# A fused streaming-encoder block: seven products for 34 more weight units

## The chip, the cores and the metric

One core of one Trainium2 chip runs the whole kernel. The time is device microseconds from one launch, as the median of several runs. TensorE does the matrix products into PSUM, the accumulator memory, which this kernel uses as four tiles of 2 x 512 float32 columns for each partition. VectorE, ScalarE and GpSimd do elementwise work, and the queue of SyncE (SP) issues the loads and stores. Each engine works through its own instructions in a fixed order and waits on semaphores where it needs another engine's result.

## The reference

The reference is one encoder layer over 256 tokens of 2048 channels, all float32:

```python
x = x + 0.5 * swiglu(rms_norm(x, ffn1_norm), ffn1_w_gate, ffn1_w_up, ffn1_w_down)   # 2048 -> 5632 -> 2048
h = rms_norm(x, mix_norm); proj = h @ w_in                # pool group, and gated linear attention
x = x + concatenate([y_pool, y_gla]) @ w_out              # 2048 x 2048
x = x + mem_cross_attention(rms_norm(x, xattn_norm), rms_norm(mem, mem_norm), w_q, w_kv, w_o)
x = x + 0.5 * swiglu(rms_norm(x, ffn2_norm), ffn2_w_gate, ffn2_w_up, ffn2_w_down)
out = rms_norm(x, final_norm)

def swiglu(h, w_gate, w_up, w_down):
    return (silu(h @ w_gate) * (h @ w_up)) @ w_down
```

Some 417 MB are read from memory, nearly all of it weights, each once.

## The kernel before

Every weight matrix is cut into **units** of 1 MB (128 partitions x 2048 float32). A unit is loaded into a buffer `raw` (three of them); ScalarE rounds it to `wh` (line 228) and VectorE makes the remainder `wl = raw - wh` (line 229). Both are in the type fp32r, and there are three buffers of each. Activations are held as a high and a low part too: `xs` (the normed input) and `ys` (what goes into the next product). A float32 product is the sum of three: high x high, high x low, low x high (`products`, line 307).

The class `Stream` writes down the order of the work: units, and between them operations with a delay in units ("after 6 more units"). `emit` splits weights two units ahead of the products and issues the load three units ahead. A scheduler then fixes each engine's order of instructions; so it may place a matmul of a later unit before one of an earlier unit, or a cast ahead of an eviction.

A unit of a wide product (`wwide`) is two 128-row chunks of the weight by 1024 columns. With 256 tokens that is a 2 x 2 block product: 2 token halves, 2 chunks of the contraction, 2 column halves, three matmuls each, so 24 matmuls of 128x512. `block_t` does just that. It holds two PSUM tiles. `block_s` does some units of a block, the *pairs* 0, 2 and 4 of eight, by a scheme with **seven** instead of eight block products (Strassen-Winograd; `seven`, line 401): 21 matmuls. For these,

- `add_weights` (lines 363 to 367) makes four sums of the unit's quarters in `T`, and `split_seven` splits the 1536 columns of `raw` that are still needed (`xh`, `xl`) and the 2048 of `T`;
- `part_sums` (lines 346 to 356) makes four sums of the activation's quarters, split into `xe`;
- four PSUM tiles are held; two of them collect the four partial products P1, P5, P6, P7, which `combine` (lines 443 to 448) adds up in an SBUF tile `sg`, and the other two collect what belongs to the output directly; `join` (line 452) adds the two, from PSUM.

Before, `block_s` is used for the gate and up columns of both feed-forward networks except the first block and the odd last column (18 blocks, 54 units of seven products). The odd column's gate and up go together through `block_t` (`wtwo`). The down products, and the products with `w_out` and `w_o`, go through `into_x`: it fetches the residual `x` from memory (`fetch_x`), runs two blocks `block_t`, adds the product to `x` (line 608), stores it, and, where a norm follows, `fold` transposes `x` on TensorE (line 621) and writes the next `xs` (lines 210, 211). The feed-forward network runs in three parts of 4, 4 and 3 columns of 512; gated columns are transposed by `turn` (line 691) into `ys` and split (lines 234, 235). The very last down product has its own form, `down_end`, with line 1188.

Of the kernel before, what the change touches and what calls it, by code (L numbers as in the profile page):

```python
# [14 lines left out]
P = 128  # L15
# [77 lines left out]
def build(ctx, tc, I, out):  # L93
# [247 lines left out]
    def part_sums(act, ext, i, g):  # L341

        t = scope["pool"].tile([P, 4 * NB], F32, tag="T", name=uid("T"))
        a = t[:, :NB].rearrange("p (k s) -> p k s", k=2)
        e = t[:, NB : 2 * NB].rearrange("p (n s) -> p n s", n=4)
        nc.vector.tensor_tensor(
            out=a, in0=f32(act[:, 2 * g : 2 * g + 2, 0, :]), in1=f32(act[:, 2 * g : 2 * g + 2, 1, :]),
            op=ALU.add,
        )
        a11, a21, a12, a22 = (a[:, k, h * P : (h + 1) * P] for k in range(2) for h in range(2))  # L350
        nc.vector.tensor_tensor(out=e[:, 3], in0=a11, in1=a21, op=ALU.subtract)
        nc.vector.tensor_tensor(out=e[:, 1], in0=a22, in1=a21, op=ALU.subtract)
        nc.vector.scalar_tensor_tensor(
            out=e[:, 2], in0=e[:, 1], scalar=-1.0, in1=a11, op0=ALU.mult, op1=ALU.subtract
        )
        nc.vector.tensor_tensor(out=e[:, 0], in0=a12, in1=e[:, 2], op=ALU.add)
        split(ext[:, i, 0], ext[:, i, 1], e)
# [27 lines left out]
    def seven(banks, act, ext, i, g, first, later, weights):  # L385
# [3 lines left out]
        n4, n1, s2, s3 = ([ext[:, i, p, n] for p in range(2)] for n in range(4))  # L389
# [6 lines left out]
        order = ("P1", "P7", "P5", "P6", "P2", "P3", "P4") if first else (  # L396
            "P1", "P2", "P3", "P7", "P5", "P6", "P4")
        for n in order:
            (a, b), wh, wl = table[n]
            for j, (x, w) in enumerate(((a, wh), (a, wl), (b, wh))):  # L400
                nc.tensor.matmul(  # L401
                    banks[n], x, w, start=first and j == 0,
                    stop=not later and n in ("P1", "P5", "P6", "P7") and j == 2,
                )

    def block_s(srcs, act, ext, pairs, evict, delays=(0, 0)):

        held, n = {}, len(srcs)

        def open_banks():  # L410
            a, b, c, d = (ptile(uid("pt")) for _ in range(4))
            held["ps"] = (d, c)
            held["parts"] = (a, b)
            held["banks"] = {
                "P1": a[:, 0], "P6": a[:, 1], "P7": b[:, 0], "P5": b[:, 1],
                "P2": c[:, 0], "P4": c[:, 1], "P3": d[:, 0],
            }

        def unit_s(g):
            def fn(weights):  # L420
                if g == pairs[0]:
                    open_banks()
                seven(held["banks"], act, ext, pairs.index(g), g, g == pairs[0], g != pairs[-1],
                      weights)
            return fn

        def unit_p(g):
            def fn(wh, wl):
                wh, wl = (w.rearrange("p (k j n) -> p k j n", j=2, n=NB) for w in (wh, wl))
                for j in (1, 0):  # L430
                    for h in range(2):
                        for kk in range(2):

                            fresh = (j, h) == (0, 1) and g == min(set(range(n)) - set(pairs)) and kk == 0
                            products(held["ps"][j][:, h, :], act, 2 * g + kk, h, wh[:, kk, j],
                                     wl[:, kk, j], fresh, g == n - 1 and kk == 1)
            return fn

        def combine():
# [8 lines left out]
            nc.vector.tensor_tensor(out=e[:, 3], in0=b[:, 1], in1=e[:, 1], op=ALU.add)  # L448

        def join(j):  # L450
            e = held["e"][:, 0:2] if j else held["e"][:, 2:4]
            nc.vector.tensor_tensor(  # L452
                out=e, in0=held["ps"][j], in1=e, op=ALU.add if j else ALU.subtract
            )
            evict(j, e)

        for g, src in enumerate(srcs):
            if g in pairs:
                st.unit(src, unit_s(g), split_seven, add_weights)
                if g == pairs[-1]:  # L460
                    st.op(combine)
            else:
                st.unit(src, unit_p(g))
        for j in (1, 0):
            st.op(lambda j=j: join(j), delays[j])
# [138 lines left out]
    def residual(scale, b):  # L604

        def evict(j, ps):
# [4 lines left out]
            if j:  # L611
                store_x(b)
        return evict

# [15 lines left out]
    def into_x(w, act, scale, gain=None, k0=0, nk=KT, spread_too=True, src=None):  # L630

        for b in range(2):
            st.op(lambda b=b: fetch_x(b, src), 2)
            block_t(wwide(w, b * 2 * NB, k0, nk), act, residual(scale, b))
# [10 lines left out]
    PAIRS = (0, 2, 4)  # L645

    def pair_sums(g, delay):
        def f():
            if g == PAIRS[0]:
                rows["xe"] = scope["pool"].tile(  # L650
                    [P, len(PAIRS), 2, 4, P], F32R, tag="xe", name=uid("xe")
                )
            part_sums(xs, rows["xe"], PAIRS.index(g), g)
        st.op(f, delay)

    class Ext:


        def __getitem__(self, i):
            return rows["xe"][i]  # L660

    def ffn(wg, wu, wd, down):
        gate = {}

# [21 lines left out]
        def turn(g, k):  # L686
# [7 lines left out]
            split(ys[:, k : k + 4, 0, :], ys[:, k : k + 4, 1, :], v)  # L694

        for lo, n in FF_PARTS:
            for b in range(0, n - 1, 2):
                n0 = (lo + b) * NB
                if lo == b == 0:
                    block_t(wwide(wg, n0), xs, lambda j, ps: ev_gate(j, ps, 1))  # L700
                else:
                    block_s(wwide(wg, n0), xs, Ext(), PAIRS, lambda j, c: ev_gate(j, c, 0))
                block_s(wwide(wu, n0), xs, Ext(), PAIRS, ev_up)
                held = {}
                st.op(lambda held=held: held.update(gate))
                wait = PAIRS[-1] + 2 if b + 2 < n - 1 else 1
                for j in range(2):
                    st.op(lambda j=j, b=b, held=held: turn(held[j], 4 * (b + j)), wait)
            if n % 2:
                def both(j, ps):  # L710
                    if j:
                        ev_up(0, ps)
                    else:
                        ev_gate(0, ps, 1)
                block_t(wtwo(wg, wu, (lo + n - 1) * NB), xs, both)
                st.op(lambda n=n: turn(gate[0], 4 * (n - 1)), 1)
            down(wd, 4 * lo, 4 * n, lo + n == FF // NB)
# [10 lines left out]
    def down_first(wd, k0, nk, last):  # L728
        into_x(wd, ys, 0.5, G_MIX if last else None, k0, nk, src=None if k0 else I["x"][0])

    for g in PAIRS:
        pair_sums(g, 5)
    ffn(I["ffn1_w_gate"][0], I["ffn1_w_up"][0], I["ffn1_w_down"][0], down_first)
# [284 lines left out]
    st.op(open_scope("s_x"), 1)  # L1018


    xa = {}
# [33 lines left out]
    into_x(I["w_out"][0], ys, 1.0, G_X)  # L1055
# [80 lines left out]
    into_x(w_o, ys, 1.0, G_FFN2, spread_too=False)  # L1136
    st.op(close_scope, 1)
    st.op(open_scope("s_ffn2"), 1)
# [8 lines left out]
    def down_last(wd, k0, nk, last):  # L1147
        if last:
            down_end(wd, k0, nk)
        else:  # L1150
            into_x(wd, ys, 0.5, None, k0, nk)
# [86 lines left out]
    for n, g in enumerate(PAIRS):  # L1238
        pair_sums(g, 3 + n)
# [70 lines left out]
```

## Time and profile before

| | |
|---|---|
| median of 3 runs | 2134.21 us (2133.54 to 2135.17) |
| the profiled execution's own time | 2133.11 us |
| its span, first to last instruction | 2131.2 us |
| TensorE matmul busy | 2111.3 us (99%), 10032 instructions |
| weight load into TensorE (PEld) | 1768.5 us (83%) |
| VectorE busy | 1427.7 us (67%) |
| ScalarE busy | 1008.0 us (47%) |
| moved by DMA | 435.91 MB, mean 205 GB/s |

Rows of the timeline give the start, then the duration, then engine, line, operation and output<-inputs, with the idle time before it and what ended that in brackets. Rows of the groups give the count, then busy time and mean duration, then idle time before them. A matmul's duration in these rows is a modelled latency (0.39 us), while the distance from one matmul's start to the next is shorter; matmuls overlap. The same holds for VectorE: a row's duration is some 0.08 us longer than its distance to the next.

### The profile page before, as it was taken

Reading aid. Unit: us, or ns where it says so; the run is one execution under the profiler, and the core shown is the slowest. Engines: PE = TensorE matmul, PEld = TensorE weight load, DVE = VectorE, ACT = ScalarE, POOL = GpSimd, SP = SyncE. Lnnn points to the kernel's source line nnn. Section 1 sums busy time; section 2 is a strip of 40 time slices with the busy share of each in tenths; the row PEclk is TensorE's granted clock in tenths of the full one; section 3 lists DMA queues with packets and bytes.
Section 4 is the critical chain, followed back from the end, with each engine's and each line's share of the span. In section 5 each row is a group of like instructions: output and inputs, shape, how many; then the busy total and the mean of one; then the engine's idle time right before and its main releaser. Section 6 shows DMA issues by size and latency. Waiting matters only on the chain.

```text
span 2131.2 us, 24070 instructions
## 1 busy us (share of the span) xinstructions
PE 2111.3 (99%) x10032; PEld 1768.5 (83%) x10032; DVE 1427.7 (67%) x1189; ACT 1008.0 (47%) x890; POOL 14.2 (1%) x41
## 2 busy tenths in 40 slices
PE   9999999999999999999999999999999999999998
PEld 7878888888888888888888888888888888888886
DVE  8876588856864576565666454567874888658744
ACT  7554354534534545455445443445443455434433
POOL 0000000000000000000000000000000000000001
PEclk9999999999999999999999999999999999999999
DMA  7556665566656655557654555666576665766663
GB/s 277 197 189 234 224 221 195 186 233 226 227 178 234 221 162 180 167 185 278 222 190 161 167 169 171 195 207 207 175 247 217 214 209 175 249 212 223 221 217 119
DMA packets 143316, 435.91 MB, mean 205 GB/s; under 512 B 9828, under 2 KB 13000, under 8 KB 142824
## 3 DMA queue, kind: packets, MB, share of 16 engines
q1 hardware_dynamic: 143176, 434.38, 60.5%
q8 instruction: 78, 1.28, 0.2%
q14 instruction: 30, 0.25, 0.0%
q10 hardware_dynamic: 32, 0.01, 0.0%
HBM read 417.58 MB, written 16.78 MB: 204 GB/s over the span
## 4 chain that ended last, share of the span: by engine, by line
PE 98%; DVE 1%; issue 0%; ACT 0%; DMA 0%; SPq 0%; DVEq 0%; ACTq 0%
PE pt L307 58%; PE pa L292 15%; PE pt L401 12%; PE pb L307 6%; PE pe L307 3%; PE ph L691 1%; PE pl L1084 1%; PE pv L1119 1%; PE px L621 0%; DVE wl L229 0%; ACT wh L228 0%; DMA x<-in_x 0%; PE px L575 0%; PE po L954 0%; PE pa L832 0%
## 5 line engine op out<-in xcount | busy, mean ns | idle before, releaser
L229 DVE TENSOR_TENSOR wl<-raw,wh 128x2048 fp32r<-128x2048 f32 (+2 forms) x328 | 740.2, 2258 | 544.5 <-ACT wh L228 543.9
L228 ACT CAST wh<-raw 128x2048 fp32r<-128x2048 f32 (+2 forms) x328 | 618.5, 1886 | 721.7 <-PE pt L307 490.5
L307 PE MATMUL pt<-wh,xs 128*128 128x512 f32 x1952 | 618.6, 390 | 0.0
L307 PE MATMUL pt<-wh,ys 128*128 128x512 f32 x1728 | 534.7, 389 | 0.0
L307 PEld LDWEIGHTS pt<-wh,xs 128*128 128x128 f32 x1952 | 366.6, 188 | 75.7
L307 PE MATMUL pt<-wl,xs 128*128 128x512 f32 x976 | 380.8, 390 | 0.0
L307 PEld LDWEIGHTS pt<-wh,ys 128*128 128x128 f32 x1728 | 324.1, 188 | 67.0
L307 PE MATMUL pt<-wl,ys 128*128 128x512 f32 x864 | 336.3, 389 | 0.0
L292 PE MATMUL pa<-xs,wh 128*128 128x512 f32 x896 | 317.1, 398 | 2.1 <-DVE t L266 1.7
L292 PE MATMUL pa<-xs,wl 128*128 128x256 f32 x896 | 248.8, 281 | 0.0
L307 PEld LDWEIGHTS pt<-wl,xs 128*128 128x128 f32 x976 | 183.5, 188 | 37.9
L292 PEld LDWEIGHTS pa<-xs,wh 128*128 128x128 f32 x896 | 167.7, 188 | 41.2 <-issue 2.0
L307 PEld LDWEIGHTS pt<-wl,ys 128*128 128x128 f32 x864 | 162.2, 188 | 33.5
L292 PEld LDWEIGHTS pa<-xs,wl 128*128 128x128 f32 x896 | 169.2, 189 | 1.6 <-issue 0.2
L228 ACT CAST wh<-T 128x2048 fp32r<-128x2048 f32 x54 | 103.3, 1912 | 135.6 <-DVE T L367 93.3
L229 DVE TENSOR_TENSOR wl<-T,wh 128x2048 fp32r<-128x2048 f32 x54 | 123.6, 2288 | 65.3 <-ACT wh L228 65.3
L307 PE MATMUL pb<-wh,xs 128*128 128x512 f32 x384 | 121.7, 392 | 0.5 <-DVE ys L211 0.5
L401 PE MATMUL pt<-wh,xe 128*128 128x512 f32 x324 | 108.7, 389 | 0.0
L229 DVE TENSOR_TENSOR xl<-raw,xh 128x1536 fp32r<-128x1536 f32 x54 | 94.5, 1750 | 2.7 <-ACT xh L228 2.7
L228 ACT CAST xh<-raw 128x1536 fp32r<-128x1536 f32 x54 | 79.9, 1479 | 28.9 <-PE pt L401 28.8
L307 PEld LDWEIGHTS pb<-wh,xs 128*128 128x128 f32 x384 | 72.0, 188 | 15.6 <-DVE ys L211 0.7
L401 PE MATMUL pt<-xh,xs 128*128 128x512 f32 x216 | 78.6, 389 | 1.7 <-DVE sg L452 1.7
(203 smaller groups left out, 1666.3 us busy)
## 6 DMA issues: line engine op xcount, KB each, us to landing
raw<-in_ffn_w_down SPq DMA_DIRECT2D x88, 1024.0 KB, 5.5
raw<-in_ffn_w_up SPq DMA_DIRECT2D x80, 1024.0 KB, 5.0
raw<-in_ffn_w_gate SPq DMA_DIRECT2D x77, 1024.0 KB, 5.0
raw<-in_w_in SPq DMA_DIRECT2D x32, 1024.0 KB, 5.2
raw<-in_xattn_w_kv SPq DMA_DIRECT2D x32, 1024.0 KB, 5.2
raw<-in_w_out SPq DMA_DIRECT2D x16, 1024.0 KB, 6.2
raw<-in_xattn_w_q SPq DMA_DIRECT2D x16, 1024.0 KB, 5.2
raw<-in_xattn_w_o SPq DMA_DIRECT2D x16, 1024.0 KB, 5.6
```

The lines of the kernel that those rows point to most:

```text
L228: in_turn("scalar", lambda: nc.scalar.copy(hi, src))
L229: in_turn("vector", lambda: nc.vector.tensor_tensor(out=lo, in0=src, in1=f32(hi), op=ALU.subtract))
L292: nc.tensor.matmul(o, w, x, start=k == 0 and i == 0, stop=last and i == 1)
L307: nc.tensor.matmul(ps, a, w, start=first and i == 0, stop=last and i == 2)
L401: nc.tensor.matmul(banks[n], x, w, start=first and j == 0, stop=not later and n in ("P1", "P5", "P6", "P7") and j == 2,)
L691: nc.tensor.transpose(v[:, i, h * P : (h + 1) * P], g[:, h, i * P : (i + 1) * P], ident)
L1084: nc.tensor.matmul(ps[:, t, :M], ys[:, 4 * h + d, a, tok], xa["K"][:, d, b, :], start=i == 0, stop=i == 11,)
L1119: nc.tensor.matmul(ps[:, d, :S], xa["V"][:, m, a, col], xa["PT"][:, m, b, :], start=i == 0, stop=i == 5,)
```

## The change

`into_x` and the odd columns go through `block_s` too. In each of the 14 blocks of `into_x` two units have seven products (`Y_PAIRS`, pairs 0 and 2), in each of the two odd columns three: 14 x 2 + 2 x 3 = 34 units more, 88 in all. Which units come when is now given by a list: `ORDER` keeps the three at places 0, 2 and 4 of a block, `Y_ORDER` puts the two at 2 and 4, `Y_FIRST` (first block of `w_out` and `w_o`) at 4 and 6.

The sums of the activations become a class `Sums`. One of the four, S3, is written into `act` itself, over a quarter that the seven products do not read; the other three go to a tile of 3 planes instead of 4. For `ys` in the feed-forward networks, `turn` calls it with the transposed columns still in PSUM, which ScalarE copies; for `w_out` and `w_o` the sums are made from `ys`. In `into_x` the combined partial products are added to `x` by `early_parts`, two more operations of 128x1024, and `join` then adds the directly collected tiles as before. `w_out` and `w_o` have scopes of SBUF memory of their own, and the load and norm of `mem` comes after `w_out` instead of during it.

```diff
-    def part_sums(act, ext, i, g):
...
+    class Sums:
...
+        def make(self, g, src=None):
+            act, i = self.act, self.pairs.index(g)
+            if i == 0:
+                self.tile = scope["pool"].tile(
+                    [P, len(self.pairs), 2, 3, P], F32R, tag=self.name, name=uid(self.name)
+                )
+            a, e = jtile(), jtile().rearrange("p (n s) -> p n s", n=4)
+            k = slice(2 * g, 2 * g + 2)
+            if src is None:
+                nc.vector.tensor_tensor(
+                    out=a.rearrange("p (k s) -> p k s", k=2), in0=f32(act[:, k, 0, :]),
+                    in1=f32(act[:, k, 1, :]), op=ALU.add,
+                )
+            else:
+                nc.scalar.copy(a.rearrange("p (k s) -> p k s", k=2), src)
+            b = a.rearrange("p (n s) -> p n s", n=4)
+            nc.vector.tensor_tensor(
+                out=e[:, 0:2], in0=b[:, 0:4:3], in1=b[:, 1:2].to_broadcast([P, 2, P]), op=ALU.subtract
+            )
+            nc.vector.scalar_tensor_tensor(
+                out=e[:, 2], in0=e[:, 1], scalar=-1.0, in1=b[:, 0], op0=ALU.mult, op1=ALU.subtract
+            )
+            nc.vector.tensor_tensor(out=e[:, 3], in0=b[:, 2], in1=e[:, 2], op=ALU.add)
+            split(self.tile[:, i, 0], self.tile[:, i, 1], e[:, 1:4])
+            split(act[:, 2 * g, 0, P:], act[:, 2 * g, 1, P:], e[:, 0])
...
-    def block_s(srcs, act, ext, pairs, evict, delays=(0, 0)):
+    def block_s(srcs, act, sums, order, evict, merge=None):
...
+        def open_whole():
+            if "ps" not in held:
+                c = banks("P2", "P4")
+                held["ps"] = (banks("P3", "P0"), c)
+        def open_parts():
+            held["parts"] = (banks("P1", "P6"), banks("P7", "P5"))
...
+            if merge is not None:
+                merge(e[:, 2:4], e[:, 0:2])
         def join(j):
+            if merge is not None:
+                evict(j, held["ps"][j])
+                return
...
+    def early_parts(scale, b):
+        def merge(minus, plus):
+            for j, e, s in ((1, plus, scale), (0, minus, -scale)):
+                x = x_cols((2 * b + j) * NB, NB)
+                nc.vector.scalar_tensor_tensor(
+                    out=x, in0=e, scalar=s, in1=x, op0=ALU.mult, op1=ALU.add
+                )
+        return merge
...
-            block_t(wwide(w, b * 2 * NB, k0, nk), act, residual(scale, b))
+            block_s(wwide(w, b * 2 * NB, k0, nk), act, sums, orders[b], residual(scale, b, 0),
+                    early_parts(scale, b))
...
-    PAIRS = (0, 2, 4)
+    PAIRS, Y_PAIRS = (0, 1, 4), (0, 2)
+    ORDER = (0, 2, 1, 3, 4, 5, 6, 7)
+    Y_FIRST = (1, 3, 4, 5, 0, 6, 2, 7)
+    Y_ORDER = (1, 3, 0, 4, 2, 5, 6, 7)
+    CLEAR = 6
...
             split(ys[:, k : k + 4, 0, :], ys[:, k : k + 4, 1, :], v)
+            if not last:
+                for g in range(k // 2, k // 2 + 2):
+                    if g in Y_PAIRS:
+                        y_sums.make(g, v[:, 2 * g - k : 2 * g - k + 2])
...
-                block_t(wtwo(wg, wu, (lo + n - 1) * NB), xs, both)
+                block_s(wtwo(wu, wg, (lo + n - 1) * NB), xs, x_sums, ORDER, both)
...
+    def out_product(name, w, gain, spread_too):
+        sums = Sums("ye", ys, Y_PAIRS)
+        st.op(open_scope(name), 1)
+        for g in Y_PAIRS:
+            st.op(lambda g=g: sums.make(g), 1)
+        into_x(w, ys, 1.0, gain, spread_too=spread_too, sums=sums, orders=y_orders(KT, Y_FIRST))
+        st.op(close_scope, 1)
+    out_product("s_out", I["w_out"][0], G_X, True)
     st.op(open_scope("s_x"), 1)
...
     st.op(mem_norm, 6)
-    into_x(I["w_out"][0], ys, 1.0, G_X)
...
-    into_x(w_o, ys, 1.0, G_FFN2, spread_too=False)
     st.op(close_scope, 1)
+    out_product("s_o", w_o, G_FFN2, False)
```

147 lines of the change are left out of this document (70 added, 77 removed).

## The prediction

> **What bounds the kernel now.** I read the page's busy shares and the chain that ended last first.
>
> ```profile
> PE 2111.3 (99%) x10032; PEld 1768.5 (83%) x10032; DVE 1427.7 (67%) x1189; ACT 1008.0 (47%) x890; POOL 14.2 (1%) x41
> PE 98%; DVE 1%; issue 0%; ACT 0%; DMA 0%; SPq 0%; DVEq 0%; ACTq 0%
> ```
>
> TensorE is the bound: 98% of the chain. Its busy time alone would not prove that, as matmuls overlap, so the next view is its timeline in an up block.
>
> ```profile
> 312.56 0.39 PE L307 MATMUL pt<-wh,xs 128*128 128x512 f32 x1
> 312.79 0.39 PE L401 MATMUL pt<-xh,xs 128*128 128x512 f32 x1
> ...
> 317.32 0.39 PE L307 MATMUL pt<-wl,xs 128*128 128x512 f32 x1
> ```
>
> From 312.56 to 317.32 lie 21 starts (rows with x2 count twice): 4.76/21 = 0.2267 us for each matmul, in plain units and in seven-product units alike. Behind the start, what distances exceed that sums to under 9 us in the whole trace, the longest being 1.7 us idle. So each matmul removed is worth 0.2267 us where the operands keep coming. Whether they do is up to VectorE, which splits the weights. Its groups, then its timeline where it is tightest:
>
> ```profile
> L229 DVE TENSOR_TENSOR xl<-raw,xh 128x1536 fp32r<-128x1536 f32 x54 | 94.5, 1750 | 2.7 <-ACT xh L228 2.7
> L608 DVE SCALAR_TENSOR_TENSOR x<-pt,x 128x1024 f32<-128x1024 f32 x28 | 34.0, 1218 | 0.6
> ```
> ```profile
> 402.53 0.68 DVE L366 TENSOR_TENSOR T<-T,raw 128x512 f32<-128x512 f32 x1
> 403.25 0.69 DVE L367 TENSOR_TENSOR T<-T,raw 128x512 f32<-128x512 f32 x1
> 405.99 2.29 DVE L229 TENSOR_TENSOR wl<-T,wh 128x2048 fp32r<-128x2048 f32 x1 [2.05 <-ACT wh L228]
> 408.20 2.28 DVE L229 TENSOR_TENSOR wl<-raw,wh 128x2048 fp32r<-128x2048 f32 x1
> 410.40 1.22 DVE L363 TENSOR_TENSOR T<-raw 128x1024 f32<-128x1024 f32 x1
> 411.54 1.75 DVE L229 TENSOR_TENSOR xl<-raw,xh 128x1536 fp32r<-128x1536 f32 x1
> 413.21 0.68 DVE L366 TENSOR_TENSOR T<-T,raw 128x512 f32<-128x512 f32 x1
> 416.67 2.29 DVE L229 TENSOR_TENSOR wl<-T,wh 128x2048 fp32r<-128x2048 f32 x1 [2.05 <-ACT wh L228]
> ```
> ```profile
> 420.91 0.39 PE L401 MATMUL pt<-wl,xe 128*128 128x512 f32 x1
> ```
>
> From start to start an operation costs VectorE 2.20 us (2048 columns), 1.67 (1536), 1.13 (1024), 0.60 (512), some 0.4 (256) and 0.2 (128). In each seven-product unit it also idles up to 2.05 us while ScalarE casts `T`. The split that ends at 418.96 is first used at 420.91: a **lead** of 1.95 us, the smallest of its kind. In the down blocks the lead is 6.67 us.
>
> The last place is the end of the first network, where the product's last column must pass into the next `xs`:
>
> ```profile
> PE pt L401 <- DVE sg L452: 1.7, 1, 1.7
> ```
> ```profile
> 723.01 2.51 DVE L608 SCALAR_TENSOR_TENSOR x<-pt,x 128x1024 f32<-128x1024 f32 x2
> ```
> ```profile
> 729.74 1.91 PE L621 MATMUL px<-ident,x 128*128 128x128 f32 x16
> 731.40 0.48 PE L292 MATMUL pa<-xs,wh 128*128 128x512 f32 x1
> ```
>
> `x` was ready 4 us before the transposes asked for it. The first line is the only wait of TensorE for a PSUM tile in the 18 blocks with seven products.
>
> **The change, part by part.** *Removed:* 34 x 3 = 102 matmuls (the instruction order has 9978 before and 9876 after): 102 x 0.2267 = **-23.1 us**, all on the path.
>
> *VectorE's new work in a down block of 8 units:* for each of two units 1.13 + 0.60 + 0.60 + 1.67 = 4.0 us; `combine` 0.60 + 1.13 + 0.60 = 2.3; merge 2 x 1.13 = 2.3. With 8 splits (17.6) and two evictions (2.3) that is 32.5 us, and 36.6 with two waits of 2.05, against TensorE's 6 x 24 + 2 x 21 = 186 matmuls, 42.2 us. It fits, so it costs 0; without that cover it would be the 12.6 us new in each block. The same holds for `w_out` and `w_o` with their folds (8 x 0.4 = 3.2 more). ScalarE gets 34 x 1.4 + 16 x 0.5 + the sums, some 70 us on 1008: hidden, at 51%.
>
> *Sums of `ys`, 14 of them:* about 0.4 + 0.2 + 0.2 + 0.45 + 0.2 = 1.5 us of VectorE each, two to a part; in four places (parts one and two of both networks) they stand in front of the tight up block. In the new order they stand just where VectorE idled 2.05 us for the cast; two waits take the 3.0 us. Ends: 0, and 3.0 each = 12.0 with the idle time filled by nothing. I take 0, by the nearest row (the 2.05 us). Behind them in VectorE's queue are the splits of the next units, for which TensorE waits.
>
> *The odd columns:* 8 splits 17.6, three seven-product units 12.0, `combine` 2.3, join and gating of the block before 5.0: 36.9, and 43.0 with three waits, against 183 matmuls and 16 transposes, 43.1 us. Break-even: 0.
>
> *Down of 6 units in the first network's third part,* two blocks: 32.7 and 30.0 us of VectorE by the same prices with turns, sums and fold, plus two waits each: 36.8 and 34.1 against TensorE's 32.2 and 33.0. Overrun 5.7, against a lead of up to 6.7 at the start. The second block's splits stand behind eight operations of the fold, and following them in the new order the last plain unit's split comes 1.8 us late. I take **+1.8**; ends 0 and 5.7.
>
> *The boundary to `w_in`.* In the new order the twelve matmuls each of the last two seven-product units on P1, P5, P6, P7 stand behind nearly all of the last unit, because the folds hold the two PSUM tiles. So `combine` starts at the product's end E. Behind it, in VectorE's order: 0.60, 1.13, a split 2.20 (for which its cast ends at E + 1.9), 0.60, merge 1.13, split 2.20, 1.13, evictions 1.13 + 1.13: `x` is ready at E + 11.5. TensorE's two next units take 2 x 5.64, so the 16 transposes (1.66 from start to start) end at E + 13.2. ScalarE then has three squares (0.61 each), a cast (1.9), another square, and only then the scaled cast of `xs` (0.45): from E + 11.5 to 16.4. VectorE has one more split (2.20) in between, behind that cast, and reaches its part of `xs` at E + 18.1. TensorE's whole rest is queued behind that unit's first matmul. Before, it would start at E + 12.9: **+5.2**. Ends: 0 (if the scheduler's order proves earlier at `combine`) and 10.4 (if the other two norm boundaries did half as much each; there three plain units follow the last seven-product unit, and `x` is ready by E + 2.3, so I take 0).
>
> *Restart of TensorE after that wait.* The trace has two rows: after 1.70 us idle the next matmuls are 0.31 and 0.24 us apart; after the 4.13 us at the start they are 0.58, 0.42, 0.43, 0.43 and 0.41 apart, 1.1 us over five normal ones. The wait here, 5 us, is nearer the second: **+1.1**; ends 0 and 1.1. The granted clock reads 1.00 in both. [...]
>
> *PSUM.* All 16 new blocks hold four tiles, where `block_t` held two. One opening in 18 waited 1.7 us: 16/18 x 1.7 = **+1.5**; ends 0 and 16 x 1.7 = 27.2.
>
> *Moves at nothing.* The residual is needed from the merge on, not from the block's end; its load (5.6 us to landing) has three units, 16 us, ahead of it, and the weight load behind it in SP's queue waits for a later split anyway. The number of transfers is the same. Without cover: 5.6 each. The load and norm of `mem` fall among `w_q` units, where VectorE has one 2.2 us split per 5.64 us. The sums of `xs` in the first block move from its start to its end, where the lead is over 4 us; writing S3 must wait for the plain products, long done. Each at 0, with 1 us either way for the first block.
>
> *Sum:* -23.1 + 1.8 + 5.2 + 1.1 + 1.5 = -13.5, against the profiled execution's 2133.1 (2.0 beside its span): 2119.6. It lies 1.1 under the median of the runs shown, so **2120.7 us**.
>
> [...]
>
> **The rivals.** *All hidden* (2111.1): no term but the removal. For it, leads over 4 us nearly everywhere; against it, the order at the `w_in` boundary. 0.13. *VectorE's waits add up* (2125 to 2137, middle 2130): in the four tight up blocks new sums do not fall into idle time, 1.05 to 4.1 us each on top of the forecast. For it, a lead of only 1.95 there; against it, the order. 0.14. *PSUM openings, the slower one* (2146.4): every new block's opening waits like the one at 1.7 us: 2120.7 - 1.5 + 27.2. For it, four tiles of four are held and the transposes need two; against it, seventeen blocks in which nothing waits, and the new order, which puts products later rather than letting them wait. It decides from 12 of 16. 0.08. *No removal* is excluded by the count of instructions.
>
> **How the numbers follow.** The forecast's own case, 0.60, runs from 2115 to 2126. Within 0.2% (4.3 us, about what a measurement can tell from no change) is 2129.9 to 2138.5. Faster: 0.60 + 0.13 + the lower half of 0.14 + half of the 0.04 that no case holds = 0.82. Same: the upper half of 0.14, and 0.01 = 0.08. Slower: 0.08 + 0.02 = 0.10. The range 2111.5 to 2133 leaves out half of the case *all hidden* (0.06) below, and 0.08 + 0.02 and a third of 0.14 above.
>
> **What would show it.** Right: 102 matmuls fewer at the same 0.2267 us; an idle time of some 5 us of TensorE before the first `pa` matmul behind the transposes of `w_in`'s start, released by VectorE's `xs` of line 211; VectorE near 80%. Wrong: `pt` matmuls waiting for `wl` or for `x`/`sg` evictions at many block starts; or no idle time at the boundary.

## The result and the profile after

The changed kernel takes 2158.26 us (median of 4 runs, 2157.03 to 2158.75) against 2133.88 us of the kernel before: a ratio of 1.0113, 95% interval 1.0095 to 1.013. It is 24.4 us slower, where 2120.7 was forecast. The profiled execution took 2158.07 us, with a span of 2156.3. The page's busy times and the chain that ended last:

```profile
PE 2112.2 (98%) x9930; PEld 1755.8 (81%) x9930; DVE 1652.3 (77%) x1479; ACT 1073.9 (50%) x984; POOL 15.2 (1%) x41
PE 82%; DVE 11%; issue 3%; ACT 2%; DMA 1%; SPq 0%; DVEq 0%; ACTq 0%
```

The 102 matmuls are gone (10032 to 9930), and VectorE's busy share (77%) is near the forecast. But VectorE has 11% of the chain, where it had 1%. TensorE's busy time has not fallen, though 102 matmuls are gone: some 13 of those 23 us came back because matmuls ran at half clock (below), and a row's modelled 0.39 us covers part of each short wait.

To find the place I took each block's length from both traces (from the first matmul of its first unit to the first of the next block's), and compared the difference with 0.2267 us for each matmul removed there. Six of the sixteen new blocks agree to 0.01 us (8-unit down and output blocks: 6 matmuls, 1.36 us each). So the removal is worth what was forecast, 23.1 us, and 48.7 us are lost elsewhere. In parts one and two of a network the blocks are gate, up, gate, up (so the third is a gate block, the fourth an up block) and two down blocks of eight units; part three has gate, up, the odd column and two down blocks of six. The rest of `w_in` reaches to the first matmul of `w_out`. The table has the loss by place, with that of four of the runs below, in us, from one profiled execution each (that of the last column took 2125.71 us, 4.5 above its median):

| where | after | sums left out | joins behind, with T | xl behind T | same, third part plain |
|---|---|---|---|---|---|
| third blocks (gate) of the parts two | 8.0 | 5.8 | 0.0 | 0.0 | 0.0 |
| two odd blocks | 5.9 | 7.0 | 0.1 | 0.1 | 0.1 |
| four fourth blocks (up) | 6.5 | 3.6 | 16.5 | 4.4 | 4.5 |
| eight 8-unit down blocks | 5.5 | 1.4 | 0.7 | 0.7 | 0.7 |
| the networks' other blocks | 0.6 | -0.1 | 5.3 | -2.1 | -1.2 |
| third part's down (first network), start of `w_in` | 9.9 | 11.2 | 12.8 | 10.4 | -0.4 |
| rest of `w_in` | 1.5 | 0.0 | 1.5 | 0.0 | 1.6 |
| `w_out`, `w_q`, `w_kv` | 8.6 | 7.2 | 7.0 | 2.7 | 4.5 |
| `w_o` | 2.1 | 2.1 | 2.1 | 2.1 | 3.8 |
| all | 48.7 | 38.3 | 46.0 | 18.4 | 13.5 |

48.7 less 23.1 is 25.6; the spans differ by 25.1, as the last block, which the table leaves out, is 0.45 us shorter.

About 26 us are lost inside the two networks, where the prediction had put nothing but some of its 1.5 us for PSUM openings. The clearest place is the third block of the first network's part two, units 64 on; the kernel before had a lead of 6.77 us there, from the end of its first split from `T` (VectorE) to the first matmul that reads it (TensorE):

```profile
346.12 2.29 DVE L229 TENSOR_TENSOR wl<-T,wh 128x2048 fp32r<-128x2048 f32 x1
355.17 0.39 PE L401 MATMUL pt<-wl,xe 128*128 128x512 f32 x1
```

VectorE's timeline of the changed kernel, and TensorE's first matmul that reads the split of 351.46; 1.13 us are left:

```profile
350.32 1.23 DVE L496 TENSOR_TENSOR sg<-pt,sg 128x1024 f32<-128x1024 f32 x1 [3.24 <-PE pt L307]
351.46 2.28 DVE L229 TENSOR_TENSOR wl<-T,wh 128x2048 fp32r<-128x2048 f32 x1
353.66 1.41 DVE L729 SCALAR_TENSOR_TENSOR sg<-sg,Rcol,sg 128x512 f32<-128x512 f32 x2
354.99 2.29 DVE L229 TENSOR_TENSOR wl<-raw,wh 128x2048 fp32r<-128x2048 f32 x1
357.19 1.22 DVE L496 TENSOR_TENSOR sg<-pt,sg 128x1024 f32<-128x1024 f32 x1
358.32 1.75 DVE L229 TENSOR_TENSOR xl<-raw,xh 128x1536 fp32r<-128x1536 f32 x1
359.99 1.22 DVE L388 TENSOR_TENSOR T<-raw 128x1024 f32<-128x1024 f32 x1
361.12 1.41 DVE L729 SCALAR_TENSOR_TENSOR sg<-sg,Rcol,sg 128x512 f32<-128x512 f32 x2
362.45 0.69 DVE L391 TENSOR_TENSOR T<-T,raw 128x512 f32<-128x512 f32 x1
363.17 0.69 DVE L392 TENSOR_TENSOR T<-T,raw 128x512 f32<-128x512 f32 x1
365.91 2.29 DVE L229 TENSOR_TENSOR wl<-T,wh 128x2048 fp32r<-128x2048 f32 x1 [2.05 <-ACT wh L228]
```
```profile
354.88 0.39 PE L426 MATMUL pt<-wl,xs 128*128 128x512 f32 x1
```

Two things are to be seen. The join (L496) of the block before waits 3.24 us for TensorE, while the split `wl` that TensorE needs next (at 354.88) stands behind it in VectorE's queue. And the split `xl` and the gating (L729) stand in front of the sums `T`, so that ScalarE can cast `T` only when VectorE has nothing else to do meanwhile: another 2.05 us idle. ScalarE is blocked by the same order, with the plain casts of the next units queued behind its cast of `T`:

```profile
363.97 1.91 ACT L228 CAST wh<-T 128x2048 fp32r<-128x2048 f32 x1 [11.69 <-DVE T L392]
365.78 1.90 ACT L228 CAST wh<-raw 128x2048 fp32r<-128x2048 f32 x1
```

And TensorE, two short waits, and then each matmul 0.43 us from the next instead of 0.2267:

```profile
365.93 0.50 PE L426 MATMUL pt<-wh,xs 128*128 128x512 f32 x1 [0.62 <-ACT wh L228]
...
367.74 0.50 PE L307 MATMUL pt<-wh,xs 128*128 128x512 f32 x1 [0.83 <-ACT wh L228]
368.26 0.63 PE L426 MATMUL pt<-wl,xs 128*128 128x512 f32 x1
368.69 0.63 PE L426 MATMUL pt<-wh,xs 128*128 128x512 f32 x1
369.12 0.63 PE L426 MATMUL pt<-wh,xe 128*128 128x512 f32 x1
```

The same stretch by windows (PE, PEld, DVE, ACT and POOL busy with their counts, then the granted clock, DMA's share and GB/s): the clock is 0.50 for just one window of 3.4 us behind the waits.

```profile
365.10:368.50 3.40, 1.93 (x6) 0.91 (x6) 2.59 (x2) 3.40 (x3) 0.00 (x0) 1.00 0.86 299
368.50:371.90 3.40, 3.40 (x9) 2.62 (x9) 3.40 (x3) 0.56 (x1) 0.00 (x0) 0.50 0.17 25
371.90:375.30 3.40, 3.40 (x16) 2.80 (x16) 2.60 (x3) 0.65 (x1) 0.00 (x0) 1.00 0.78 287
```

The changed kernel has eight such windows inside, the kernel before none. In each some 7 matmuls of 15 are lost, 1.6 us, together some 13 of the 48.7 us.

Over the whole trace, the waits (us in all, times, longest), of which the kernel before had 93.3 us (26 times) of the first kind, ScalarE's for `T`, none of the second and third, and one of 1.7 us of the fourth:

```profile
ACT wh L228 <- DVE T L392: 302.8, 61, 11.7
DVE sg L496 <- PE pt L307: 15.0, 5, 3.2
PE pt L307 <- ACT wh L228: 5.6, 6, 1.3
PE pt L426 <- DVE sg L496: 3.5, 4, 1.7
```

and VectorE's group of the splits from `T`, before and then after; the number behind the second bar is its idle time in front of them:

```profile
L229 DVE TENSOR_TENSOR wl<-T,wh 128x2048 fp32r<-128x2048 f32 x54 | 123.6, 2288 | 65.3 <-ACT wh L228 65.3
```
```profile
L229 DVE TENSOR_TENSOR wl<-T,wh 128x2048 fp32r<-128x2048 f32 x88 | 201.6, 2291 | 112.8 <-ACT wh L228 112.8
```

At the boundary to `w_in`, TensorE's timeline shows the waits that the prediction had worked out, and one more, for the PSUM tile that `combine` (L483) frees:

```profile
730.30 0.50 PE L292 MATMUL pa<-xs,wh 128*128 128x512 f32 x1 [1.76 <-DVE sg L483]
...
747.77 0.80 PE L292 MATMUL pa<-xs,wh 128*128 128x512 f32 x1 [3.75 <-DVE xs L211]
```

### The profile page after: what moved, and what is told of

Read it like the earlier page. It is cut to its first block, busy times and chain, and to the rows that moved or that the text cites. A ratio compares the mean times of both kernels' runs of the same rounds, so it can differ in the third digit from the quotient of the medians.

```text
span 2156.3 us, 24303 instructions
## 1 busy us (share of the span) xinstructions
PE 2112.2 (98%) x9930; PEld 1755.8 (81%) x9930; DVE 1652.3 (77%) x1479; ACT 1073.9 (50%) x984; POOL 15.2 (1%) x41
## 4 chain that ended last, share of the span: by engine, by line
PE 82%; DVE 11%; issue 3%; ACT 2%; DMA 1%; SPq 0%; DVEq 0%; ACTq 0%
PE pt L307 40%; PE pt L426 16%; PE pa L292 14%; PE pb L307 6%; DVE wl L229 4%; PE pe L307 3%; ACT wh L228 2%; DVE xl L229 2%; DVE sg L496 1%; DVE T L388 1%; DVE sg L729 1%; DMA raw<-in_ffn_w_down 1%; DVE T L391 1%; PE pl L1151 1%; PE pv L1186 1%
## 5 line engine op out<-in xcount | busy, mean ns | idle before, releaser
L229 DVE TENSOR_TENSOR wl<-raw,wh 128x2048 fp32r<-128x2048 f32 (+2 forms) x294 | 661.1, 2253 | 283.7 <-ACT wh L228 283.0
L228 ACT CAST wh<-raw 128x2048 fp32r<-128x2048 f32 (+2 forms) x294 | 552.0, 1882 | 424.2 <-PE pt L307 162.5
L307 PE MATMUL pt<-wh,xs 128*128 128x512 f32 x1856 | 595.8, 391 | 3.3 <-ACT wh L228 3.3
L307 PE MATMUL pt<-wh,ys 128*128 128x512 f32 x1280 | 405.6, 392 | 2.3 <-ACT wh L228 2.3
L228 ACT CAST wh<-T 128x2048 fp32r<-128x2048 f32 x88 | 168.3, 1912 | 326.2 <-DVE T L392 302.8
L229 DVE TENSOR_TENSOR wl<-T,wh 128x2048 fp32r<-128x2048 f32 x88 | 201.6, 2291 | 112.8 <-ACT wh L228 112.8
L307 PEld LDWEIGHTS pt<-wh,ys 128*128 128x128 f32 x1280 | 241.8, 189 | 54.4 <-ACT wh L228 3.4
L307 PE MATMUL pt<-wl,ys 128*128 128x512 f32 x640 | 250.8, 392 | 3.9 <-DVE wl L229 3.9
L229 DVE TENSOR_TENSOR xl<-raw,xh 128x1536 fp32r<-128x1536 f32 x88 | 154.3, 1753 | 0.0
L388 DVE TENSOR_TENSOR T<-raw 128x1024 f32<-128x1024 f32 x88 | 107.4, 1221 | 8.8 <-DMA raw<-in_ffn_w_down 7.2
L426 PE MATMUL pt<-wh,xs 128*128 128x512 f32 x240 | 95.0, 396 | 2.4 <-ACT wh L228 2.4
```

Of the source, the lines that this page charges most:

```text
L228: in_turn("scalar", lambda: nc.scalar.copy(hi, src))
L229: in_turn("vector", lambda: nc.vector.tensor_tensor(out=lo, in0=src, in1=f32(hi), op=ALU.subtract))
L307: nc.tensor.matmul(ps, a, w, start=first and i == 0, stop=last and i == 2)
L388: nc.vector.tensor_tensor(out=v[:, 0:2], in0=w[:, 1:3], in1=w[:, 0:1].to_broadcast([P, 2, NB]), op=ALU.add)
L426: nc.tensor.matmul(banks[n], x, w, start=n in fresh and j == 0, stop=n in ends and j == 2)
```

## The experiments

**The theories.** *A:* the order in VectorE's queue costs the time; in its later form *A'*, that VectorE idles for the cast of `T`, because `xl` is split ahead of `T`. *B:* VectorE has too much to do in these blocks. *C:* four PSUM tiles of four are held, and openings wait. *D:* the sums of `ys` cost nothing.

**Joins behind the splits.** In `block_s`:

```
+        def behind(j):
+            with tc.issue_after(latest["vector"].ins):
+                join(j)
+
...
-            st.op(lambda j=j: join(j))
+            st.op(lambda j=j: behind(j))
```

> The changed kernel, with both joins of every seven-product block (and the evictions made with them) queued on VectorE behind the split of the second unit after the block. Theory A (the order in VectorE's queue): the changed kernel loses 19.9 us in six blocks (3.99 + 1.83 in the third and fourth blocks of the first network's second part, 2.95 in its odd block, 4.01 + 4.10 and 2.97 in the second network) because a join that waits for TensorE stands in front of the next block's weight split; with the joins behind the splits most of it comes back: 2138 to 2146 us. Theory B (VectorE has too much work: 77% busy against 67%): the same operations in another order change nothing: 2155 to 2160 us. Theory C (four PSUM tiles of four are held): later joins free the tiles later, 16 openings wait longer: slower than 2160 us.

Measured: 2151.02 us (two runs, 2148.89 and 2153.15; ratio to before 1.0082, 1.0062 to 1.0102), 7.2 below the changed kernel and between the ranges of A and B. The two third blocks lose 3.2 us instead of 8.0, the two odd blocks 3.3 instead of 5.9, so the order counts; but less came back than A said, and the fourth blocks lose 7.6 instead of 6.5. The idle time in front of the splits from `T` is still there (122.4 us in all).

**Joins behind the sums T as well.** `behind` also waits its turn behind the last add of `add_weights`.

```
...
-        nc.vector.tensor_tensor(out=v[:, 3], in0=v[:, 2], in1=w[:, 3], op=ALU.add)
+        latest["adds"] = nc.vector.tensor_tensor(out=v[:, 3], in0=v[:, 2], in1=w[:, 3], op=ALU.add)
...
+            with tc.issue_after(latest["vector"].ins), tc.issue_after(latest["adds"].ins):
```

> As the kernel with the joins behind the splits, and behind the sums of raw weights T of the next seven-product unit as well, so that the cast of T on ScalarE and the casts queued behind it no longer wait for the gating. Theory A: another 2 to 5 us on top of the kernel with the joins behind the splits alone: 2134 to 2142 us. Theory B: 2155 to 2160 us. Theory C (tiles, or raw weights that come late hold the joins): slower than the kernel with the joins behind the splits alone, with waits of TensorE for sg at block openings.

Measured: 2153.63 us (ratio to before 1.0091, 1.0074 to 1.0108). The third and odd blocks now lose nothing (0.1 us in all four). But the fourth blocks, where the sums of `ys` and the turns fall, lose 16.5 us, and there it is theory C: in three of the four, which lose 4.9 us each, TensorE waits 2.34 us for a tile, and a window at half clock follows (in the block below the matmuls start some 0.43 us apart from 1565.97 to 1569.37). TensorE's row and then VectorE's in the fourth block of the second network's part one:

```profile
1564.70 0.50 PE L426 MATMUL pt<-xh,xs 128*128 128x512 f32 x1 [2.34 <-DVE sg L496]
```
```profile
1562.82 0.68 DVE L392 TENSOR_TENSOR T<-T,raw 128x512 f32<-128x512 f32 x1
1563.43 2.35 DVE L496 TENSOR_TENSOR sg<-pt,sg 128x1024 f32<-128x1024 f32 x2
```

The joins come only after all the sums, and the new block's tiles wait for them. So a join too early holds up splits, and one too late holds up PSUM. VectorE's idle time in front of the splits from `T` fell from 112.8 to 69.5 us in this run, and the loss only from 48.7 to 46.0: the sum of the idle time does not set the time, its place does.

**The same, with the third part's down product plain.**

```
-            block_s(wwide(w, b * 2 * NB, k0, nk), act, sums, orders[b], residual(scale, b, 0),
-                    early_parts(scale, b))
+            if not (scale == 0.5 and nk == 12):
+                block_s(wwide(w, b * 2 * NB, k0, nk), act, sums, orders[b], residual(scale, b, 0),
+                        early_parts(scale, b))
+            else:
+                block_t(wwide(w, b * 2 * NB, k0, nk), act, residual(scale, b))
...
-            end = last and lo + n == FF // NB
+            end = lo + n == FF // NB
```

> As the kernel with the joins behind the splits and the sums of weights, and the third part's down product of the first network (two blocks of six units, four seven-product units) plain as before. That gives 12 matmuls back, 2.7 us. The prediction's terms of that place measured 5.0 + 1.3 us in the two blocks and 4.9 us at the boundary to w_in. If these come from the seven-product units there, the time is 6 to 9 us below the kernel before it: 2127 to 2134 us. If they come from elsewhere (the folds, the order), it is 2.7 us above it.

Measured: 2143.66 us, 10.0 below the kernel with the same joins. The time that was expected, 2127 to 2134 us, was missed, because it was counted from a faster kernel than the one before it proved to be; the difference, 6 to 9 us, was nearly met. The 12.8 us lost at the six-unit blocks and the start of `w_in` are gone (less 2.7 for the 12 matmuls put back, that is 10.1): they belong to the four seven-product units there.

**None of the 34 units.** Odd columns, down and output products by `block_t`, no sums of `ys`. (The odd columns read `xs`, in which S3 already stands in place of A21, so they compute something else.)

> The changed kernel with none of the 34 new seven-product units: odd columns, down and output products as before, no sums of the activations; what stays of the change is the new set of pairs of the gate and up blocks and their order (0, 2, 1, 3, ...), in which seven-product units stand in the same positions as before, S3 kept in xs, and the sums with fewer operations. Theory A (order): in VectorE's written-out order the join of the block before stands in front of the first split of the third block of part two in this kernel too, so the loss in those blocks shows without any new unit: 3.99 + 1.83 + 4.01 + 4.10 = 13.9 us, 2145 to 2150 us, slower than the kernel before although it has the same 10032 matmuls. Theory B (VectorE's amount of work): VectorE has no more to do than before: 2133 to 2136 us.

Measured: 2136.83 us; ratio 1.0016 (1.0006 to 1.0027). The premise of theory A was mistaken here: in this kernel's written-out order the joins stand behind the splits, as in the kernel before, and no block of the networks loses more than it did before. So the run does not set A against B; it shows that the new pairs and their order cost the networks nothing. What it lost in its trace is 1.6 us in a window at half clock (910.3 to 913.7, between the products of `w_in` and `w_out`) and a wait for `xs` at the start of `w_q` (1.92 us idle, 2.1 by the starts).

**Only the odd columns.** Their six units by `block_s`; down and output products plain.

> Of the 34 new seven-product units only the six of the two odd columns; the down and output products are plain as in the kernel before, and no sums of the activations are made. 18 matmuls fewer than before are worth 18 x 0.2267 = 4.1 us. In this kernel's written-out order the joins before the odd columns stand behind the splits wl of the first two units, where in the changed kernel they stand in front of the first. Theory A (order): the odd blocks lose at most 0.5 us each, 2129 to 2131 us. Theory B (the odd block's own work on VectorE, 43.0 us with three waits against 43.1, is too much): each loses about 3 us, as in the changed kernel: 2134 to 2137 us.

Measured: 2131.79 us; ratio 0.9991 (0.9982 to 1.0001). The odd blocks are 2.02 and 1.99 us shorter, of 2.04 possible: with the joins behind the splits "break-even" costs nothing, and theory B falls for these blocks. The whole can't be told from the kernel before; it is 0.8 us above what A expected, because the start of `w_q` lost 4.4 us, where the load of `mem` was moved to. ScalarE's queue, then TensorE's, in this run:

```profile
1035.96 0.42 ACT L244 ACTIVATE j<-mem 128x256 f32<-128x256 f32 x1 [2.25 <-DMA mem<-in_mem]
...
1036.37 1.89 ACT L228 CAST wh<-raw 128x2048 fp32r<-128x2048 f32 x1
1038.16 0.83 ACT L210 ACTIVATE xs<-px,gains 128x256 fp32r<-128x256 f32 x2
```
```profile
1041.04 0.78 PE L292 MATMUL pa<-xs,wh 128*128 128x512 f32 x1 [2.59 <-DVE xs L211]
```

A square of `mem` waits for its transfer, and behind it stand the cast of weights and the scaled `xs` that TensorE needs.

**The sums of ys left out.**

```
+                if self.name == "ye":
+                    nc.gpsimd.memset(f32(self.tile), 0.5)
+            if self.name == "ye":
+                return
```

> The changed kernel without the sums of the activations ys: the 14 calls that make them are left out, the tile that they fill holds a constant and S3 isn't written, so down and output products with seven products compute something else; all other operations and all matmuls stay. In its written-out order the joins stand in front of the splits at the same places as in the changed kernel (third block of the parts two, odd blocks). Theory A (order): the 3.99 + 4.01 + 2.95 + 2.97 = 13.9 us lost there remain, and only what falls where sums stand goes (1.83 and 1.33 in the first network, 3.83 and 4.10 in the second, 0.57: 11.7 us): 2145 to 2150 us. Theory B (amount of VectorE's work): 14 x 1.5 to 2.0 us less in just these places gives the leads back in all of them: 2132 to 2140 us. Theory D (sums are hidden, as the prediction had it): 2156 to 2160 us.

Measured: 2148.55 us (two runs, 2147.52 and 2149.57), in theory A's range: the third and odd blocks lose 12.8 us still (13.9 before), although VectorE has 22.5 us less to do (1629.8 against 1652.3); the fourth and the down blocks lose 5.0 instead of 12.0. So in this order the sums cost some 7 us, and theory D falls too. They cost it in this order only: with `xl` behind `T` (below) the same blocks lose 5.1 us with all the sums in place.

**xl behind T.** Both edits together: the joins behind the splits, and in each seven-product unit

```
-        split_weights(*r, raw[:, NB:])
+        with tc.issue_after(added[u].ins):
+            split_weights(*r, raw[:, NB:])
```

where `added[u]` is the last add of the unit's `T`; only VectorE's `xl` is moved by it.

> The joins behind the splits, and in each seven-product unit the split xl of the raw weights queued on VectorE behind the sums T, so that ScalarE casts T while VectorE splits xl; VectorE's idle time of up to 2.05 us in each of these units should go. Theory A' (VectorE's queue is short of time where sums of ys, joins and T meet, and its waits for the cast are what it lacks): the losses in the gate, up and odd blocks and in the 8-unit down blocks go nearly all; those at the boundaries stay (5.0 + 1.3 in the six-unit down blocks, 4.9 at w_in, some 8.7 at w_out and w_q, 2.1 at w_o): 2132 to 2138 us. Theory C (tiles): openings wait for the later joins as in the run with the joins behind the splits alone, 2148 us and more.

Measured: 2129.88 us; ratio 0.9981 (0.9971 to 0.999). 28 us come back with not one operation less, more than A' had said.

**Odd and output products.**

> Odd columns and the two output products with seven products, the down products plain and no sums in the networks. 42 matmuls fewer than before: 9.5 us. If the loss at w_out, w_q and w_o (2.5 + 6.2 + 2.1 = 10.8 us in the changed kernel) is made there, by the folds that hold two PSUM tiles and put the seven-product units late in TensorE's order, it is here as well: the run with the odd columns alone minus 5.4 plus 10.8, some 2135 to 2137 us. If it is carried over from elsewhere, 2124 to 2126 us.

Measured: 2136.53 us, 4.7 above the odd columns alone, though 24 matmuls (5.4 us) fewer. `w_out`'s second block loses 3.0, the start of `w_q` 6.2 (4.4 of it there with the odd columns alone), `w_o`'s second block 3.7: the loss is made there, not carried over.

**xl behind T alone.** Without the forced joins.

> The changed kernel with one edit: the split xl of a seven-product unit is queued on VectorE behind the sums T of the same unit; the joins aren't forced. In the order that the scheduler then writes, the joins stand behind the splits of the next two units by themselves. Theory A' (the split xl in front of T makes VectorE wait for the cast of T, 2.05 us in each such unit, and the rest of the order follows from it): as the run with both edits, 2127 to 2133 us. Rival (the forced joins were what helped, and xl little): 2140 to 2152 us.

Measured: 2129.03 us; ratio 0.9984 (0.9974 to 0.9993), the same as with both. It had to be: the rows of VectorE, ScalarE and TensorE follow in the same order in both traces, so this is a second measurement of one order, in which the joins stand behind the splits either way. What `xl` adds is shown by two runs above: the joins behind `T` without it, 2153.63 us, and with it, 2129.88. The joins in front and `xl` behind `T` were not run. The page's busy times and chain, and VectorE's group of splits from `T`:

```profile
PE 2095.0 (99%) x9930; PEld 1749.8 (82%) x9930; DVE 1653.1 (78%) x1479; ACT 1080.3 (51%) x984; POOL 15.2 (1%) x41
PE 95%; DVE 3%; ACT 1%; issue 1%; DMA 0%; DVEq 0%; ACTq 0%
```
```profile
L229 DVE TENSOR_TENSOR wl<-T,wh 128x2048 fp32r<-128x2048 f32 x88 | 201.2, 2286 | 23.8 <-ACT wh L228 23.4
```

VectorE is as busy as in the changed kernel (1653.1 against 1652.3), and the networks, but for the third part, lose 3.1 us where they lost 26.5. In the kernel before, `xl` stood in front of the last add of `T` in 22 of 54 units, with 2.07 us of idle time behind it on average; in the changed kernel in 66 of 88, with 1.60; here in none, and 89 us of idle time are gone. The edit has a price too: of the 4.4 us still lost in the fourth blocks 3.2 fall in three of them, in each of which TensorE now waits 0.53 to 0.56 us for an `xl`. The start of the block shown above, now, and TensorE's first matmul that reads the split of 342.68:

```profile
339.81 0.68 DVE L394 TENSOR_TENSOR T<-T,raw 128x512 f32<-128x512 f32 x1
340.41 0.68 DVE L490 TENSOR_TENSOR sg<-pt,sg 128x512 f32<-128x512 f32 x1
341.01 1.75 DVE L229 TENSOR_TENSOR xl<-raw,xh 128x1536 fp32r<-128x1536 f32 x1
342.68 2.28 DVE L229 TENSOR_TENSOR wl<-T,wh 128x2048 fp32r<-128x2048 f32 x1
...
350.38 1.22 DVE L499 TENSOR_TENSOR sg<-pt,sg 128x1024 f32<-128x1024 f32 x1
```
```profile
351.73 0.39 PE L429 MATMUL pt<-wl,xs 128*128 128x512 f32 x1
```

VectorE splits `xl` while ScalarE casts `T`, goes on without a gap, and the join follows by itself, with nothing to wait for. The split `wl` ends at 344.96 and is first used at 351.73: a lead of 6.77 us again, as in the kernel before, where the changed kernel has 1.13.

**And the third part plain.** The edit shown above, on this kernel.

> As the kernel with xl behind T alone, and the third part's down product of the first network plain, without its sums: 12 matmuls back (2.7 us), against 4.5 us in its second block, 6.3 at the boundary to w_in and 1.5 of a half-clock window behind it that the run with both edits showed. If these belong to the seven-product units there: 8 to 9.5 us below the kernel with xl alone, 2119 to 2124 us. If to the order elsewhere: 2.7 above it.

Measured: 2121.17 us; ratio 0.9947 (0.9932 to 0.9962), 7.9 below. Of the 34 units 30 stay. By the medians it is 0.6% below the kernel before and 1.7% below the changed one.

**mem four units later,** `st.op(mem_norm, 10)` for 6.

> As the kernel before it, with the norm of mem four units later (after ten units of w_q instead of six). In the run with the odd columns alone ScalarE waited 2.25 us for the transfer of mem at the start of w_q, with the casts of xs and wh queued behind it, and TensorE lost 2.6 us and a half-clock window (4.4 us in all); the prediction put that move at nothing. If that wait stands in this kernel too, 2 to 4.4 us come back: 2116 to 2120 us. If the order here already hides it, as in the run with both edits (0.7 us lost there): within 1 us of the kernel before it.

Measured: 2123.90 us; ratio 0.9953 (0.9939 to 0.9968), no difference from the run before it that can be told. The start of `w_q` lost 0.8 us in both: here the order hides that transfer.

**Later sevens in the outputs' second blocks.** `orders=[list(Y_FIRST), list((1,3,4,0,5,2,6,7))]`.

> As the kernel before it, and in the second block of w_out and of w_o the seven-product units one and two positions later (order 1, 3, 4, 0, 5, 2, 6, 7), so that the folds of the first block have given back their two PSUM tiles before the four partial products are opened. If the 2.1 us lost in each of these two blocks come from the folds holding the tiles: 3 to 4 us less, 2113 to 2118 us. If the later units only push the products that wait toward the end (the boundary effect of w_in): 2 to 6 us more.

Measured: 2128.73 us; ratio 0.9975 (0.9964 to 0.9985), 4.8 slower. The second thing expected happened: the start of `w_q` lost 4.6 us and that of the second network 6.0, of which 5.7 are only moved there from `w_o`'s second block. At `w_q` TensorE waits 2.85 us for `xs`, as at `w_in`. The premise of the first thing is not borne out either: in the kernel before it TensorE's one long wait in each of these second blocks, 1.59 us, is for a split `wl` (996.24 and 1385.21), not for a tile.

**The same edit on the kernel before.** xl behind T, nothing else.

> The kernel before (no new seven-product unit) with the edit of the kernel with xl behind T alone: the split xl of each of its 54 seven-product units queued on VectorE behind the sums T. If the edit gives back only what the changed kernel lost through its order (TensorE waits under 9 us in the whole kernel before, 1.7 us of it at the second block of the first network), the time is that of the kernel before less 0 to 2 us: 2131 to 2134 us. If VectorE's waits for the cast (65.3 us of idle time in the kernel before) cost TensorE there as well, 2120 to 2130 us.

Measured: 2131.82 us; ratio 0.9987 (0.9978 to 0.9996). It gains some 2 to 3 us: the one wait for a PSUM tile (1.7 us) is gone, and 33 us of VectorE's idle time, nearly all of which cost nothing here. So of the 28 to 29 us that the edit gives the changed kernel nearly all undo a loss of that kernel's own order. Against this run, the 34 units gain 2.8 us by the medians, which the two intervals (0.9978 to 0.9996 and 0.9974 to 0.9993) don't tell from nothing, and 30 of them 10.7.

## Why the prediction was wrong

**The steps that failed** are three, with one error in them: "It fits, so it costs 0" (the 8-unit down blocks), "In the new order they stand just where VectorE idled 2.05 us for the cast; two waits take the 3.0 us" (the sums), and "Break-even: 0" (the odd columns). Measured: 12.0 us in the eight down and four fourth blocks, of which 7.0 go when the sums are left out; 5.9 in the odd blocks; and 8.0 more in the two third blocks, in which the change alters no matmul. All three sums add up VectorE's work and a number of 2.05-us waits, and compare with TensorE's time. The work was right: by the prediction's prices the new work comes to 226 us, measured are 224.6, and the same 1653 us fit when `xl` stands behind `T`. The waits were not a constant of the unit, and not room for other work. They are made by the order in the queue: 65.3 us before, 112.8 after, 23.8 with `xl` behind `T`. That the order is the cause is shown, as the same operations in another order take 29 us less. How much of it acts through the idle time and how much because `T`, its cast and the joins come later is not separated. I had read in the changed order where the sums stand; I had not read where the joins and `xl` stand, and used the leads of the kernel before ("over 4 us nearly everywhere"; in the third block 6.77 us, where 1.13 was left).

**Right:** the removal, -23.1. The place and cause at the third part and `w_in`: +1.8, +5.2 and +1.1 make 8.1, against 9.9 measured, with the chain as worked out (folds, late sevens, `combine`, residual, `xs`); the run with that product plain gets it back. The wait of 1.76 us for the tile that `combine` frees had no term. The term for the restart was too small: the window at half clock there (747.4 to 750.8) is worth 1.6 us, as in the other windows. Its second row, the start, was read wrongly: the trace's records of the clock begin only at 8.78 us, and up to 8.80 the matmuls start some 0.43 us apart, which is the distance where the changed kernel's clock reads 0.50 (0.427 us), so the 1.00 ahead of that is no reading. PSUM openings: +1.5 against 3.5 us of waits; the slower rival's 27.2 did not come, though one run shows that its mechanism is real (16.5 us in four blocks, clock included, when the joins are put late).

**Sized wrongly at one end:** the norm boundaries behind `w_out` and `w_o`, "so I take 0", with 5.2 for the two together at the other end (10.4 with `w_in`), measured 8.6 (`w_out` to `w_kv`) and 2.1 (`w_o`). The move of `mem`, 0, is 4.4 us in the run with the odd columns alone; in the changed kernel I can't separate it.

**The rivals:** *VectorE's waits add up* came nearest to the mechanism, with waits of 1.05 to 4.1 us in four tight blocks; it went wrong by the number of places and by leaving out the half-clock windows behind short waits, which cost 1.6 us each here. It put 9.3 us on top of the forecast at its middle; the networks alone lost 26. The 0.01 that the forecast's chance of *same* adds to half of the 0.14 has no run behind it: in the traces before and after the change no two long matmuls start less than 0.224 us apart, and the median is 0.227.

**Open:** why the scheduler puts the joins in front with the down products in seven products, and behind with none or with the odd columns alone, wasn't tried. Nor is it known why a `wl` comes late in the outputs' second blocks (1.59 us of waiting and a half-clock window, 3.8 us each in the best kernel), or what the rest of the 4.5 us in its fourth blocks is.

## What to carry to other kernels

A ledger of an engine's work against the bound engine's time is not enough near break-even: read, in the changed order, what stands in front of each operation that the bound engine waits for, and who waits for whom there. An idle time of an engine that waits for another's half of a pair (here a cast and its remainder) can be closed by putting work that doesn't depend on it in between, in the right order (112.8 us of it became 23.8 here). Here the products that ended late before a change of operand cost more at that boundary (9.9 us) than they saved (2.7).

## What the runs showed of the hardware

In the changed kernel's trace the records of the granted clock read 0.50 seven times inside the kernel: six records of 3.413 us, from 368.47, 747.35, 921.43, 1617.75, 1788.42 and 1825.96 us, and one of 6.827, from 1013.59. The records at 1.00 around them last 105, 110, 50, 26, 175, 49, 10 and 94 times 3.413 us; in the kernel before a single one lasts from 8.78 to 2125.04, 620 times as long. Where one long matmul follows another without a wait, they start 0.427 us apart in the records at 0.50 and 0.227 outside them (medians).

Idle time is counted here by the starts: what passes between 0.2267 us after the start of a long matmul and the next start, and not by the idle time of the rows, which begins only after the modelled 0.39 us. In the 3.413 us ahead of six of the records at 0.50 TensorE idled 2.10, 2.13, 2.20, 2.46, 2.84 and 3.41 us (in the last no matmul starts), the 2.20 in four pieces (0.78, 0.11, 1.00 and 0.30); ahead of the one from 921.43 short matmuls stand, and I have not counted it. Of all other stretches of 3.413 us that have long matmuls only, counted on from the same records, the highest idle time was 1.90 us in this trace (from 726.87) and 1.96 in the trace of the kernel before (from 138.48), and the clock read 1.00 behind both. What happens between 1.96 and 2.10, and whether the idle time alone decides, these two traces don't show.

So the length of a wait alone does not tell what it cost here: behind the wait of 1.76 us at 730.30 the clock stayed at 1.00, behind those of 0.62 and 0.83 us at 365.93 and 367.74 it read 0.50 for one record. Behind the wait of 1.59 us at 1406.59, in `w_o`'s second block, no record at 0.50 follows, and `w_o` lost 2.1 us; with the third part plain it lost 3.8, and the 1.7 more are about one such window.
